# Second fp16 copies of attention probabilities on VectorE, and sample state products in 32-column groups, in a hybrid decoder layer

## The chip, the cores and the metric

The kernel runs on one core of one Trainium2 chip. The metric is the device time of one execution in microseconds (us). A core has five engines with an instruction stream each: TensorE (PE in the profile; its weight loads are PEld), VectorE (DVE), ScalarE (ACT), GpSimd (POOL) and SyncE (SP), which here issues the transfers. They meet only at semaphores.

## The reference

One inference step of a decoder layer for a prompt of 2048 tokens and for a sample batch of 8 sequences with 8 new tokens each.

```python
h = rmsnorm(x, norm_w)
z = h @ w_in
q, k, v, qb, kb, vb, g_lr, gate_a, gate_b = jnp.split(z, split_points(), axis=-1)
q = rope(rmsnorm(heads(q, H_A), q_norm_w), pos)
k = rope(rmsnorm(heads(k, H_A), k_norm_w), pos)
o_a = attend(q, k, v)             # 8 heads of 64, windows (128,1), (512,4), (2048,16), mixed by their denominators
log_a = jax.nn.log_sigmoid((g_lr @ w_gate_up + b_gate).astype(jnp.float32)) / GATE_TAU
o_b, s_fin = gla_chunked(...)     # 4 heads, keys of 64, values of 128
o_b = rmsnorm(o_b, gla_norm_w)
mixed = jnp.concatenate([o_a * silu(gate_a), o_b * silu(gate_b)], axis=-1)
y = x + mixed @ w_out
```

Two places in it matter for the change. In the attention of the prompt each query has a softmax, p = exp(s - m), and the product of p with the values. In the gated linear attention each head carries a state of 64 x 128, and one chunk does

```python
o = (jnp.einsum('bhts,bhsv->bhtv', scores, vc)
     + jnp.einsum('bhtk,bhkv->bhtv', qc * jnp.exp(b), state))
state = (jnp.exp(b_last)[..., None] * state
         + jnp.einsum('bhsk,bhsv->bhkv', kc * jnp.exp(b_last[:, :, None] - b), vc))
```

For the sample the chunk is the 8 new tokens, and each of the 8 sequences has states of its own, which come from and go back to device memory.

## The kernel before, in words

**Projections.** The input projection goes over 16 tiles of 128 prompt rows and a tile of 64 sample rows. Rows and weights are kept as two fp16 parts each, and a product is three matmuls for each 128 of the depth (lines L1628, L1316 and L1319). These matmuls are the bulk of TensorE's work, and they are also what stands between the steps of the attention.

**Attention of the prompt.** `attend` (L888) makes one unit of work: 128 queries of two heads (branches 1 and 2, window 128 by 1 and 512 by 4) or of four heads (branch 3). A unit has three steps. In `qk` TensorE makes scores (L901), VectorE masks them and takes the maximum (L909), and ScalarE takes the exponential (L912). In `tr` TensorE transposes the probabilities (L919) into PSUM, and `split` (L873) makes two fp16 parts of them, the rounded copy h and the remainder l. In `pv` TensorE multiplies both parts with the values (L934), and `added` (L945) joins the two halves of the result with ScalarE (L950) and VectorE (L951) and stores it.

**`split`** deals with its calls in turn. On an odd call ScalarE makes h (L878) and VectorE the remainder (L879), both from PSUM. On an even call ScalarE first copies the whole tile to SBUF as fp32 (L881), then h is made from that copy, and GpSimd makes the remainder (L886). That second h is made by ScalarE (L883), or by VectorE (L885) when the count of calls is a multiple of four. Since `added` raises the count by two, 72 of the 80 second copies go to ScalarE and 8, all of branch 3, to VectorE.

**The state of the sample.** `sample_gla` (L1816) works on two pairs of heads, p = 0 and 1. A pair's states of all 8 sequences lie in S0: 128 partitions (two heads of 64) by 8 sequences by 256 columns (the two heads' values, the blocks off the diagonal zero). The queries are spread into qxs, 72 columns for each sequence with 8 filled, so that any window of 64 columns holds one sequence's queries at its own place and zeros elsewhere. Eight matmuls (L1850) add up all sequences into O_s, 64 rows by 256; two small ones for each pair add the products within the chunk (L1856). For the new states GpSimd expands the values over the sequences (L1868, tile vx) and scales the old states (L1874); TensorE makes the updates U_s (L1878), two matmuls of 512 columns for each head, and VectorE adds them (L1882). The two heads of a pair use the two column halves of TensorE's array, since their results stand on partitions 0 to 63 and 64 to 127.

**The order.** No scheduler decides what stands where. `ORDER` (L52) lists for each engine the numbers of its instructions in the order in which they are to run, and `in_order` (L545) binds them in that order. So an engine that waits for one instruction holds up all that is listed behind it. The same TensorE stream holds attention, projections and gated linear attention, listed between each other. SyncE's list sets the order in which transfers are issued. The other work of the core that runs at the same time are the scores of the sample against its cache of keys: GpSimd multiplies (L1483) and VectorE reduces (L1484).

Of the kernel before, what the change touches and what calls it, by code (L numbers as in the profile page):

```python
# [7 lines left out]
F32 = mybir.dt.float32  # L8
# [4 lines left out]
AF = mybir.ActivationFunctionType  # L13
# [5 lines left out]
P = 128  # L19
# [6 lines left out]
NS = 64  # L26
# [534 lines left out]
def tile_hymba(ctx: ExitStack, tc: tile.TileContext, A: dict):  # L561
# [277 lines left out]
    with ExitStack() as c1:  # L839
# [33 lines left out]
        def split(out, in_, f):  # L873
# [6 lines left out]
            else:  # L880
                ACT.activation(f, in_, AF.Copy, scale=P_SCALE)  # L881
                if split_[0] % 4:
                    ACT.activation(h, f, AF.Copy)  # L883
                else:
                    DVE.tensor_copy(h, f)  # L885
# [1503 lines left out]
```

## Time and profile before

| | |
|---|---|
| time, median of 3 executions | 1237.86 us (1237.41 to 1240.5) |
| the profiled execution | 1238.56 us, of which the span of the trace is 1236.7 |
| mean granted clock of TensorE | 0.998 |
| TensorE busy | 1188.1 us (96%) |
| VectorE busy | 948.1 us (77%) |
| ScalarE busy | 817.6 us (66%) |
| GpSimd busy | 542.8 us (44%) |
| moved by DMA | 283.08 MB, 229 GB/s mean |
| second fp16 copies | 72 on ScalarE, from 149.6 to 712.4 us; 8 on VectorE, from 547.8 to 722.5 us |
| state products and updates of the sample | 762.5 to about 826 us |

Shares are of the whole span. The stages overlap, and each has its own limit, so a share of the span says little about a stage; the tables by stretch of time in the prediction do. Starts are given from the start of the span. A row of the trace names line, engine, operation, the tiles written and read, and shapes as partitions by elements. An fp32 matmul leaves two rows, so L1850's 16 matmuls are 32 rows and L1878's 8 are 16.

### The profile page before, as it was taken

Reading aid. Unit: us, or ns where it says so; the run is one execution under the profiler, and the core shown is the slowest. Engines: PE = TensorE matmul, PEld = TensorE weight load, DVE = VectorE, ACT = ScalarE, POOL = GpSimd, SP = SyncE. Lnnn points to the kernel's source line nnn. Section 1 sums busy time; section 2 is a strip of 40 time slices with the busy share of each in tenths; the row PEclk is TensorE's granted clock in tenths of the full one; section 3 lists DMA queues with packets and bytes.
Section 4 is the critical chain, followed back from the end, with each engine's and each line's share of the span. In section 5 each row is a group of like instructions: output and inputs, shape, how many; then the busy total and the mean of one; then the engine's idle time right before and its main releaser. Section 6 shows DMA issues by size and latency. Waiting matters only on the chain.

```text
span 1236.7 us, 26182 instructions
## 1 busy us (share of the span) xinstructions
PE 1188.1 (96%) x8942; PEld 717.8 (58%) x8942; DVE 948.1 (77%) x2458; ACT 817.6 (66%) x2183; POOL 542.8 (44%) x475
## 2 busy tenths in 40 slices
PE   5999999999999999999999999999999999999998
PEld 3444465566666656666777665645655665555543
DVE  7988788888988958668777675689999999833562
ACT  6555697889689968968866653568878865421220
POOL 0155443565647335552444466655535454401220
PEclk9999999999999999999999999999999999999999
DMA  8658946988856898789999876865773477899971
GB/s 292 231 171 240 232 144 163 239 214 207 199 175 165 208 248 283 229 234 267 269 247 260 252 232 209 233 196 177 233 250 95 155 245 237 284 348 370 401 275 49
DMA packets 235832, 283.08 MB, mean 229 GB/s; under 512 B 116193, under 2 KB 146866, under 8 KB 232626
## 3 DMA queue, kind: packets, MB, share of 16 engines
q1 hardware_dynamic: 235698, 281.40, 76.6%
q8 instruction: 71, 1.16, 0.4%
q14 instruction: 63, 0.52, 0.1%
HBM read 183.02 MB, written 75.24 MB: 209 GB/s over the span
## 4 chain that ended last, share of the span: by engine, by line
PE 57%; DVE 17%; ACT 11%; DMA 5%; issue 5%; POOL 2%; SPq 1%; POOLq 0%; DVEq 0%; ACTq 0%
PE Y L1974 10%; PE acc_v L1628 5%; PE acc_q L1628 4%; PE acc_k L1628 4%; PE acc_gb L1628 4%; PE t L919 3%; PE acc_qkb L1628 3%; PE O L934 3%; ACT p L912 3%; PE acc_vb L1628 3%; PE s L901 3%; PE acc_g L1628 3%; DVE p L909 2%; PE OS L2231 2%; PE sc_e L745 1%
## 5 line engine op out<-in xcount | busy, mean ns | idle before, releaser
L1483 POOL TENSOR_TENSOR pr<-k,qb 128x512 f32<-128x512 f32 x128 | 167.5, 1309 | 163.3 <-DVE sck L1484 73.0
L1628 PEld LDWEIGHTS <-hr 128*128 128x128 f16 x1824 | 172.6, 98 | 111.0 <-issue 10.8
L912 ACT ACTIVATE p<-p,o 128x256 f32<-128x256 f32 (+1 forms) x384 | 172.9, 455 | 24.3 <-DVE o L909 17.6
L1628 PEld LDWEIGHTS <-hl 128*128 128x128 f16 x1248 | 119.7, 98 | 119.1 <-issue 7.5
L1974 PE MATMUL Y<-w_o,mh 128*128 128x512 f16 x768 | 180.3, 379 | 0.1
L886 POOL TENSOR_TENSOR pt<-p,pt 128x512 f16<-128x512 f32 (+1 forms) x80 | 91.2, 1140 | 125.1 <-ACT pt L883 89.0
L934 PE MATMUL O<-v,pt 128*128 128x128 f16 x1200 | 134.7, 220 | 5.0 <-DVE o L951 1.6
L1484 DVE TENSOR_REDUCE sck<-pr 128x8 f32<-128x512 f32 x128 | 87.0, 680 | 49.8 <-POOL pr L1483 49.4
L919 PE MATMUL t<-ident,p 128*128 128x128 f32 x600 | 120.2, 279 | 4.9 <-ACT p L912 2.9
L1974 PEld LDWEIGHTS <-mh 128*128 128x128 f16 x768 | 72.3, 98 | 78.6 <-issue 4.9
L934 PEld LDWEIGHTS <-pt 128*128 128x128 f16 x1200 | 94.5, 99 | 36.7 <-POOL pt L886 3.8
L1628 PE MATMUL acc_q<-w_q,hl 128*128 128x512 f16 x384 | 109.5, 379 | 1.3 <-DVE vp L1283 1.2
L1628 PE MATMUL acc_g<-w_g,hr 128*128 128x272 f16 (+1 forms) x768 | 109.5, 277 | 0.9 <-DVE so_g L1170 0.6
L1628 PE MATMUL acc_v<-w_v,hl 128*128 128x512 f16 x384 | 109.6, 383 | 0.7 <-DVE vp L1283 0.7
L1628 PE MATMUL acc_k<-w_k,hl 128*128 128x512 f16 x384 | 108.6, 379 | 1.0 <-DVE vp L1283 0.7
L1628 PE MATMUL acc_vb<-w_vb,hr 128*128 128x512 f16 x384 | 95.1, 379 | 1.5 <-DVE so_g L1170 1.5
L909 DVE CUSTOM_DVE_ANT_0 p<-s,m3w,scl_s 128x128 f32<-128x128 f32 (+1 forms) x256 | 87.1, 395 | 11.3 <-DMA o_d<-o 5.0
L1628 PE MATMUL acc_gb<-w_gb,hr 128*128 128x512 f16 x384 | 93.8, 380 | 0.0
L919 PEld LDWEIGHTS t<-ident,p 128*128 128x128 f32 x600 | 75.3, 141 | 27.0 <-ACT p L912 12.8
L901 PE MATMUL s<-kk,qq 128*128 128x256 f16 (+1 forms) x512 | 84.8, 264 | 5.0 <-DVE o L909 2.0
L1628 PE MATMUL acc_qkb<-w_qkb,hr 128*128 128x512 f16 x288 | 81.5, 379 | 0.4 <-ACT zq L1248 0.4
L2016 POOL TENSOR_TENSOR oc<-oc 128x512 f32<-128x512 f32 x32 | 39.7, 1257 | 86.1 <-DVE oc L2009 68.2
(539 smaller groups left out, 2494.8 us busy)
## 6 DMA issues: line engine op xcount, KB each, us to landing
k<-in_cache_k_win SPq DMA_DIRECT2D x104, 256.0 KB
sv_b<-in_cache_v_win SPq DMA_DIRECT2D x24, 1024.0 KB
hr<-h_d SPq DMA_DIRECT2D x44, 512.0 KB
qb<-q_d SPq DMA_DIRECT2D x64, 256.0 KB
oc<-o_d SPq DMA_DIRECT2D x48, 264.0 KB
o_d<-o SPq DMA_DIRECT2D x64, 132.0 KB
x<-in_x_prompt SPq DMA_DIRECT2D x16, 512.0 KB
h_d<-hl SPq DMA_DIRECT2D x16, 512.0 KB
```

Source lines behind the costliest of these rows:

```text
L886: POOL.tensor_tensor(l, f, h, ALU.subtract)
L901: PE.matmul(s_ps[:, i * w : (i + 1) * w], q, k, start=(n == 0), stop=(n == len(prods) - 1),)
L909: DVE.tensor_tensor_reduce(s[:, sl], s_ps[:, sl], mask, neg, BIG, ALU.add, ALU.min, nmf(i))
L912: ACT.activation(s[:, sl], s[:, sl], AF.Exp, bias=nmf(i), scale=-1.0, accum_out=denf(i))
L919: PE.transpose(p_ps[:, i * P : (i + 1) * P], t["s"][:, i * P : (i + 1) * P], ident[:])
L934: PE.matmul(o_, t["pt"][:, c, (i * nb + b) * P : (i * nb + b + 1) * P], vf(i, b), start=(n == 0), stop=(n == 2 * nb - 1),)
L1483: POOL.tensor_tensor(pr[:], kt, qt, ALU.mult)
L1484: DVE.tensor_reduce(out, pr[:].rearrange("p (u k d) -> p u k d", u=2, k=4), AX.X, ALU.add)
L1628: PE.matmul(z, a_[:, k, :], w[:, p_, k, cols], start=(k == 0 and i == 0), stop=(k == KT - 1 and i == 2),)
L1974: PE.matmul(Y[:], a_[:, k, :], w_[:, part, k, :512], start=(i == 0), stop=(i == len(prods) - 1),)
L2016: eng.tensor_tensor(o_[g], o_[g], w[:, g].unsqueeze(2).to_broadcast([P, NH, HD]), ALU.mult)
L2231: PE.matmul(OS[32 * x : 32 * x + 32, 0:256], ps(x), vs_[bb][:, 256 * u : 256 * u + 256], start=(i == 0), stop=(i == 13),)
```

## The change

There are three parts. The number of matmuls stays as it is, and so does the set of transfers.

1. In `split` the second copy h is always made by VectorE. 72 copies (62 of 128x512, 10 of 128x256) go from ScalarE's list to VectorE's.
2. In `sample_gla` the state products write 32 rows in place of 64 (four sequences each), into column group 0 or 32 of the array, and neighbours alternate between the two. qxs is cut to 512 columns for each pair, which takes two small copies more. Both heads' expanded values are made first (two buffers for vx), and the updates U_s go over the column blocks outside and the heads inside, so that neighbours alternate between the array's halves; the additions follow them.
3. `ORDER` is replaced as a whole. On all five engines neighbours move past each other by a few places; which transfers there are and what they move is as before.

```diff
             else:
                 ACT.activation(f, in_, AF.Copy, scale=P_SCALE)
-                if split_[0] % 4:
-                    ACT.activation(h, f, AF.Copy)
-                else:
-                    DVE.tensor_copy(h, f)
+                DVE.tensor_copy(h, f)
                 POOL.tensor_tensor(l, f, h, ALU.subtract)
...
-            qxs = g1.tile([P, 2, 8, 72], F32, name="qxs")
+            qxs = g1.tile([P, 2, 512], F32, name="qxs")
             POOL.memset(qxs[:], 0.0)
             for p in range(2):
                 POOL.tensor_copy(
-                    qxs[:, p, :, 0:8], qe[:, p, :].rearrange("p (b t) -> p b t", t=8)
+                    qxs[:, p, :504].rearrange("p (b s) -> p b s", s=72)[:, :, 0:8],
+                    qe[:, p, :56].rearrange("p (b t) -> p b t", t=8),
                 )
+                POOL.tensor_copy(qxs[:, p, 504:512], qe[:, p, 56:64])
...
-                qxp = qxs[:, p].rearrange("p b s -> p (b s)")
-                for bt in range(8):
-                    PE.matmul(
-                        O[:NS, p * 256 : (p + 1) * 256], qxp[:, 64 * bt : 64 * bt + 64],
-                        S0[:, bt, :], start=(bt == 0), stop=False,
-                    )
+                for i in range(4):
+                    for g in range(2):
+                        bt, r0 = 4 * g + i, 32 * g
+                        PE.matmul(
+                            O[r0 : r0 + 32, p * 256 : (p + 1) * 256],
+                            qxs[:, p, 64 * bt + r0 : 64 * bt + r0 + 32],
+                            S0[:, bt, :], start=(i == 0), stop=False, tile_position=(0, r0),
+                        )
...
+                vxs = []
                 for j in range(2):
...
-                    vx = g1.tile([NS, 8, P], F32, name=f"vx_{h}", tag="vx", bufs=1)
+                    vx = g1.tile([NS, 8, P], F32, name=f"vx_{h}", tag="vx", bufs=2)
...
+                    vxs.append(vx)
...
+                for q in range(2):
+                    for j in range(2):
+                        h = 2 * p + j
+                        PE.matmul(
+                            Us[q][64 * j : 64 * j + 64], kdt[:NS, 0, 64 * h : 64 * h + 64],
+                            vxs[j][:, 4 * q : 4 * q + 4, :], start=True, stop=True,
+                        )
+                for j in range(2):
...
                     for q in range(2):
-                        PE.matmul(
-                            Us[q][js], kdt[:NS, 0, 64 * h : 64 * h + 64],
-                            vx[:, 4 * q : 4 * q + 4, :], start=True, stop=True,
-                        )
                         DVE.tensor_tensor(
```

Of `ORDER` these are two lines of TensorE's list; all others change in the same way.

```diff
-        "898-900 388-389 393-396 400-401 909-911 916-918 407-408 412 402 413 419 403 420 424 414 425 415 "
+        "898-900 388-389 393-396 400-401 909-911 916-917 407-408 412 402 413 419 403 918 420 424 414 425 "
```

What it moves is seen best in the engines' instruction lists. Lines shift a little: a row of L878, L881, L909, L912 or L951 before is L880, L883, L908, L911 or L950 after, and the cast on VectorE is L884. First ScalarE near 152 us, in the first units of branch 1. In a name like `pt_1_0_1_3_1` the first number is the branch, the last is the pair of heads in a group of four: a 0 is an odd call of `split`, a 1 an even one; p are probabilities, t their transpose in PSUM, o the result with maximum and denominator. Before:

```order
L878 ACTIVATE pt_1_0_0_1_0_1332<-t_1_0_0_1_0_1327 128x512
L912 ACTIVATE p_1_0_0_2_0_1339,o_1_0_0_2_1318<-p_1_0_0_2_0_1339,o_1_0_0_2_1318 128x256
L881 ACTIVATE p_1_0_0_1_1_1293<-t_1_0_0_1_1_1362 128x512
L912 ACTIVATE p_1_0_0_2_0_1339,o_1_0_0_2_1318<-p_1_0_0_2_0_1339,o_1_0_0_2_1318 128x256
L883 ACTIVATE pt_1_0_0_1_1_1367<-p_1_0_0_1_1_1293 128x512
L912 ACTIVATE p_1_0_0_2_1_1375,o_1_0_0_2_1318<-p_1_0_0_2_1_1375,o_1_0_0_2_1318 128x256 x2
L950 ACTIVATE ol_5_1358<-O_1_0_0_0_1319 128x256
```

And after, the same place:

```order
L880 ACTIVATE pt_1_0_0_1_0_1332<-t_1_0_0_1_0_1327 128x512
L911 ACTIVATE p_1_0_0_2_0_1339,o_1_0_0_2_1318<-p_1_0_0_2_0_1339,o_1_0_0_2_1318 128x256
L883 ACTIVATE p_1_0_0_1_1_1293<-t_1_0_0_1_1_1362 128x512
L911 ACTIVATE p_1_0_0_2_0_1339,o_1_0_0_2_1318<-p_1_0_0_2_0_1339,o_1_0_0_2_1318 128x256
L911 ACTIVATE p_1_0_0_2_1_1375,o_1_0_0_2_1318<-p_1_0_0_2_1_1375,o_1_0_0_2_1318 128x256 x2
L949 ACTIVATE ol_5_1358<-O_1_0_0_0_1319 128x256
```

The cast is gone from between the exponentials; all else stands as it did.

Then VectorE near 194 us. ra, rv and rs belong to the norm of a row tile, za to the projection of the sample rows. Before:

```order
L951 TENSOR_TENSOR o_1_0_1_2_2051<-O_1_0_1_2_2268,ol_45_2315 128x4x64
L631 TENSOR_TENSOR ra_x10_2234<-rr_x10_2233 128x1
L627 TENSOR_SCALAR rv_x11_2578<-ss_11_2574 128x1
L632 SCALAR_TENSOR_TENSOR ra_x10_2234<-ra_x10_2234,rv_x10_2232 128x1
L633 SCALAR_TENSOR_TENSOR rs_10_2231<-ra_x10_2234,rr_x10_2233 128x1
L1330 TENSOR_TENSOR za_0_2611<-za_0_2611,acc_q_s_2594 64x512
L879 SCALAR_TENSOR_TENSOR pt_2_0_1_0_0_2373<-t_2_0_1_0_0_2367,pt_2_0_1_0_0_2373 128x256
```

After:

```order
L884 CAST pt_1_0_1_3_1_2324<-p_1_0_1_3_1_2253 128x512
L633 TENSOR_TENSOR ra_x10_2234<-rr_x10_2233 128x1
L950 TENSOR_TENSOR o_1_0_1_2_2051<-O_1_0_1_2_2268,ol_45_2315 128x4x64
L629 TENSOR_SCALAR rv_x11_2578<-ss_11_2574 128x1
L634 SCALAR_TENSOR_TENSOR ra_x10_2234<-ra_x10_2234,rv_x10_2232 128x1
L1329 TENSOR_TENSOR za_0_2611<-za_0_2611,acc_q_s_2594 64x512
L635 SCALAR_TENSOR_TENSOR rs_10_2231<-ra_x10_2234,rr_x10_2233 128x1
L884 CAST pt_2_0_1_0_1_2410<-p_2_0_1_0_1_2332 128x256
L881 SCALAR_TENSOR_TENSOR pt_2_0_1_0_0_2373<-t_2_0_1_0_0_2367,pt_2_0_1_0_0_2373 128x256
```

Two casts came in, the combination of a unit's result moved behind a step of the norm, and the sum for the sample moved ahead of another.

Last TensorE at 762 to 776 us, the first pair of heads of the sample. S0 are the states, vx the expanded values, U_s00 and U_s01 the updates of sequences 0 to 3 and 4 to 7. Before, the products stand in two pieces, with the first head's updates between them:

```order
L1628 MATMUL acc_g1_13_12212<-w_g_6885,hr_13_11627 128x256
L1850 MATMUL O_s_9879<-S0_0_9880,qxs_9875 64x256 x2
L1878 MATMUL U_s00_9894<-vx_0_9896,kdt_smp_9871 64x512
L1878 MATMUL U_s01_9895<-vx_0_9896,kdt_smp_9871 64x512
L1850 MATMUL O_s_9879<-S0_0_9880,qxs_9875 64x256 x6
L1628 LDWEIGHTS hr_13_11627
```

After, the eight products stand together some 40 rows earlier (`O_s_9881<-S0_0_9882,qxs_9875 32x256 x8`), and the updates of both heads follow as below; before, the second head's updates stood some 60 rows behind the first's, each with an L1856 after it.

```order
L670 MATMUL ptg_e0_0_10026<-ident_79,zqk_e0_10013 128x128
L1885 MATMUL U_s00_9896<-vx_0_9898,kdt_smp_9871 64x512
L1885 MATMUL U_s00_9896<-vx_1_9901,kdt_smp_9871 64x512
L1859 MATMUL O_s_9881<-vb_s_9873,Ac_smp_9675 64x128
L1885 MATMUL U_s01_9897<-vx_0_9898,kdt_smp_9871 64x512
L1885 MATMUL U_s01_9897<-vx_1_9901,kdt_smp_9871 64x512
L1859 MATMUL O_s_9881<-vb_s_9873,Ac_smp_9675 64x128
```

The two heads' updates now stand next to each other. In the second pair of heads they don't: there the updates from vx_2 stand together, and those from vx_3 some 150 rows later, as before.

More of the change, by code (lines that the diff above doesn't have):

```diff
@@ L1876, in sample_gla @@
                     )
+                for q in range(2):
[6 more added lines that the diff above has]
+                for j in range(2):
+                    h = 2 * p + j
+                    js = slice(64 * j, 64 * j + 64)
+                    sd = S0[js, :, j * P : (j + 1) * P]
                     for q in range(2):
-                        PE.matmul(
-                            Us[q][js], kdt[:NS, 0, 64 * h : 64 * h + 64],
-                            vx[:, 4 * q : 4 * q + 4, :], start=True, stop=True,
-                        )
                         DVE.tensor_tensor(
```

886 rows, old and new, of the table ORDER are left out of this document.

## The prediction

> **What bounds the kernel now.** First the busy shares and the chain that ended last, from the page:
>
> ```profile
> PE 1188.1 (96%) x8942; PEld 717.8 (58%) x8942; DVE 948.1 (77%) x2458; ACT 817.6 (66%) x2183; POOL 542.8 (44%) x475
> PE 57%; DVE 17%; ACT 11%; DMA 5%; issue 5%; POOL 2%; SPq 1%; POOLq 0%; DVEq 0%; ACTq 0%
> ```
>
> TensorE carries most of the time, and ScalarE's and VectorE's shares of the chain (11% and 17%) say that in places they hold it up. Where, is seen in a table of busy time by stretch (start, end and length; busy time of PE, PEld, DVE, ACT and POOL with instructions; granted clock, DMA share, GB/s). The casts that the change moves run from 149.6 to 722.5 us, the sample's products in 760 to 830:
>
> ```profile
> 145.00:200.00 55.00, 50.91 (x442) 34.44 (x443) 46.08 (x165) 53.38 (x181) 21.88 (x20) 1.00 0.49 156
> 200.00:300.00 100.00, 99.79 (x704) 62.05 (x703) 85.24 (x220) 83.36 (x233) 57.08 (x44) 1.00 0.90 219
> 300.00:395.00 95.00, 95.00 (x726) 63.11 (x724) 82.69 (x202) 79.93 (x226) 56.23 (x43) 1.00 0.70 183
> 395.00:455.00 60.00, 53.53 (x404) 34.09 (x401) 44.38 (x127) 47.92 (x137) 22.13 (x17) 1.00 0.90 225
> 455.00:545.00 90.00, 89.49 (x731) 62.09 (x729) 66.08 (x215) 80.80 (x244) 49.10 (x41) 1.00 0.80 239
> 580.00:725.00 145.00, 142.63 (x1191) 102.89 (x1189) 104.79 (x357) 99.06 (x342) 67.07 (x53) 1.00 0.99 254
> 760.00:830.00 70.00, 68.00 (x392) 36.62 (x389) 48.54 (x82) 35.65 (x82) 41.30 (x32) 1.00 0.70 210
> ```
>
> So there are three kinds of stretch. In 145 to 200 ScalarE is full (53.38 of 55) and TensorE is not (50.91); in 395 to 455 TensorE misses 6.5 us. From 200 to 395 and from 455 to 545 TensorE has no gap worth naming (99.79 of 100, 95.00 of 95, 89.49 of 90): there nothing done for ScalarE can pay. In 760 to 830 TensorE is busy 68.0 of 70 and its own work is the time.
>
> All sums below stand against the profiled execution, 1238.56 us, which lies 0.70 above the median of 1237.86.
>
> **1. The casts leave ScalarE.** The rows of the two casts (duration as least/median/most), and ScalarE's cast by stretch:
>
> ```profile
> L883 ACT ACTIVATE pt<-p x72: 401/629/690, 149.6 to 712.4; 128x512 f16<-128x512 f32 x62, 128x256 f16<-128x256 f32 x10
> 145.00:200.00 55.00, 6.68 (x13) 1.00 0.49 156
> 200.00:300.00 100.00, 8.14 (x14) 1.00 0.90 219
> 300.00:395.00 95.00, 8.96 (x14) 1.00 0.70 183
> 395.00:455.00 60.00, 5.01 (x8) 1.00 0.90 225
> 455.00:545.00 90.00, 10.07 (x16) 1.00 0.80 239
> 580.00:725.00 145.00, 3.74 (x6) 1.00 0.99 254
> ```
>
> Together with one cast between 545 and 580 that is all 72. What ScalarE's lateness costs TensorE is in the waits of 145 to 200 (total, times, longest):
>
> ```profile
> PEld t L919 <- ACT p L912: 3.5, 10, 0.8
> PEld L934 <- POOL pt L886: 1.8, 6, 0.4
> PEld L934 <- ACT pt L878: 1.3, 4, 0.5
> PE t L919 <- ACT p L912: 1.1, 3, 0.6
> ```
>
> These are 7.7 us of waits on the weight load and the matmul, which partly lie over each other; TensorE's gap is 55.00 - 50.91 = 4.1. All stand behind ScalarE: the exponentials (L912) and first copies (L878) queue behind the casts, and POOL's subtraction (L886) waits for a cast. Taking 13 casts out frees 6.68 us of 53.38. The wait does not vanish, though. VectorE is busy 46.08 there and receives the 13: at the mean of its eight casts (0.60, below) for six pieces of 512 columns and some 0.35, an estimate from that, for seven of 256 (so many by the listed order), 6.0 us, so 52.1 of 55. The next bound is then VectorE at 52.1, 2.9 below the stretch. I take **-2.5**; the ends are -4.1 (the whole gap) and 0 (VectorE takes the wait over).
>
> In 395 to 455 eight casts (5.01) go, and TensorE's waits for ScalarE are:
>
> ```profile
> PEld t L919 <- ACT p L912: 2.2, 8, 0.4
> PEld L934 <- ACT pt L878: 1.5, 3, 0.9
> PEld t L919 <- ACT p L881: 1.3, 2, 0.8
> PE t L919 <- ACT p L881: 0.8, 2, 0.6
> PE O L934 <- ACT pt L878: 0.7, 1, 0.7
> ```
>
> That is 6.5 with overlaps, of which not all is the casts' doing: ScalarE is busy only 47.92 of 60 and also waits for others. 5.01 of 47.92 is a tenth of its work, so between 0.7 (a tenth of the waits) and 5.0 (every cast stood in front of a wait); I take **-1.7**, nearer to the tenth. In 580 to 725 only six casts are left: **-0.3**. Sum -4.5, between 0 and -9.
>
> **2. The casts land on VectorE.** The eight that it has already, then one of them beside what GpSimd did (start, duration):
>
> ```profile
> L885 DVE CAST pt<-p x8: 418/427/1000, 547.8 to 722.5; 128x512 f16<-128x512 f32 x8
> 597.13 1.00 DVE L885 CAST pt<-p 128x512 f16<-128x512 f32 x1
> 596.57 1.28 POOL L1483 TENSOR_TENSOR pr<-k,qb 128x512 f32<-128x512 f32 x1 [0.80 <-DVE sck L1484]
> ```
>
> Five took 418 to 427 ns; the three that began while GpSimd was in a product of L1483 took longer, the one quoted from 597.13 to 598.13, 0.28 after the product's end at 597.85. The eight sum to 4.8 us, 0.60 each. In 200 to 395 VectorE holds 85.24 + 82.69 = 167.9 of 195 and gets 28 casts: 28 x 0.60 = 16.8, so 184.7 or 95%. The ends are 28 x 0.42 = 11.8 and 28 x 1.00 = 28.0, and with the latter VectorE would be at 195.9 of 195. What covers the casts there is TensorE's projection matmuls, which the listed order puts between the attention steps. How loose that cover is, shows in TensorE's waits over 200 to 395, of which these are the largest two:
>
> ```profile
> PEld t L919 <- ACT p L912: 2.0, 7, 0.4
> PEld L934 <- DVE pt L879: 0.7, 2, 0.5
> ```
>
> VectorE was late twice, 0.7 us in all. What is queued behind a cast is the masks and maxima of the next scores (L909), then ScalarE's exponential, then the transposes, which are the first row. I take **+1.0**, about the size of what VectorE costs now; with the cover gone it is all of 16.8. In 455 to 545, 16 x 0.60 = 9.6 on top of 66.08 leaves VectorE at 84% and costs nothing.
>
> A rule of the Trainium skill speaks against this move: SBUF — State Buffer, section "SBUF: two separate sides", says that VectorE in a two-port mode and GpSimd share a pair of ports as an exclusive lock, which whoever starts first keeps for the whole instruction. The trace agrees (1.00 us against 0.42). By that rule a cast meets GpSimd with GpSimd's share of this stretch, (57.08 + 56.23) / 195 = 58%, and waits half a product, 0.64, so 0.42 + 0.37 = 0.79, and 28 of them 22 us in place of 16.8: still under the 27 that VectorE has free, so the sum stays and the first rival's chance rises.
>
> **3. The sample's state products in two column groups.** The rows of the two lines (least/median/most in ns) and the matmuls in time; then, from the sample attention later, the same shape in four column groups:
>
> ```profile
> L1850 PE MATMUL O_s<-S,qxs x32: 379/379/430, 762.5 to 811.5; 128*64 128x256 f32 x32
> L1878 PE MATMUL U_s<-vx,kdt_smp x16: 589/589/640, 763.5 to 825.3; 64*64 64x512 f32 x16
> 763.53 1.93 PE L1878 MATMUL U_s<-vx,kdt_smp 64*64 64x512 f32 x4
> 765.38 2.80 PE L1850 MATMUL O_s<-S,qxs 128*64 128x256 f32 x12
> 768.12 3.19 PE L1628 MATMUL acc_vb<-w_vb,hr 128*128 128x512 f16 x14
> 773.58 0.64 PE L1878 MATMUL U_s<-vx,kdt_smp 64*64 64x512 f32 x1
> 773.59 0.43 PE L1856 MATMUL O_s<-vb_s,Ac_smp 64*64 64x128 f32 x2
> 775.44 0.39 PE L1628 MATMUL acc_vb<-w_vb,hr 128*128 128x512 f16 x1
> 1094.66 1.91 PE L2231 MATMUL OS<-sv_b,P2x 128*32 128x256 f32 x32
> 1096.38 0.83 PE L2231 MATMUL OS<-sv_b,P3x 128*32 128x256 f32 x12
> ```
>
> Twelve rows of the state product take from 765.38 to 768.12, 0.23 each (each fp32 matmul leaves two rows). With neighbours in four column groups, 32 rows of the same 128x256 take from 1094.66 to 1096.38, 0.054 each. Two groups should be half as good as four, 0.108 (an estimate from that row). 32 x (0.23 - 0.108) = **-3.9**; the ends are 0 (no overlap) and 32 x (0.23 - 0.054) = -5.6.
>
> Updates: the first two matmuls (four rows) take 763.53 to 765.38, the other two 773.58 to 775.44, and the small products L1856 begin 0.01 after an update, in the other half: halves do run side by side here. Now all four of the first pair of heads stand together in alternating halves: 1.85 + 1.86 = 3.7 becomes some 1.86 plus what of L1856 sticks out (two pairs of rows of 0.43, half hidden), 2.3: **-1.4**, ends 0 and -1.9. In the second pair of heads the four updates stay apart by half, as the order rows show, and gain nothing. The zero fill is an eighth smaller and two copies of 8 columns come in on GpSimd, which no TensorE row waits for here: nothing. Together -5.3; TensorE being busy 68.0 of 70, most passes on, and I take **-4.8** for what later waits may keep.
>
> Against it stands the Trainium skill's TensorEngine Tiling (Array Packing), "Key Properties": a change of tiling mode drains TensorE. In the two lines' rows the longest is 0.05 above the usual (430 against 379, 640 against 589 ns), which I read as what a change of kind costs, and the visits stay about as many (fewer in the first pair of heads, more in the second), so by the rule too the sum moves by some 0.1.
>
> **4. The new orders.** They move neighbours past each other on all engines and add no work. Near 194 us, as the rows show, two casts stand in front of VectorE's next steps, and its combination L951 moves behind two short steps. Nothing in the trace prices this: nearest are the waits above, single ones of 0.4 to 0.9, so I take 0 with 2 us either way.
>
> **Sum:** -4.5 + 1.0 - 4.8 = -8.3, so 1238.56 - 8.3 = 1230.3, and 1229.6 beside the median; I say **1230**.
>
> **Rivals.**
> - *VectorE becomes the bound from 200 to 395.* Its 27.1 us without work are mostly waits for others' results, so new work does not simply fall into them. If they stay, the 16.8 appears in the time: 1238.56 - 9.3 + 16.8 = **1246**. For it: 95% busy and casts of up to 1.00. Against it: TensorE, full there, waits for VectorE 0.7 in 195, so the casts have a reserve. It decides when TensorE's waits on L879, L909 and the casts' subtraction grow by over 8 us there. Chance 0.13.
> - *ScalarE's wait only changes hands*, or what is won before 455 is lost from 580 on, where the DMA share is 0.99 and rows of the cache come no sooner: only the sample pays, 1238.56 - 4.8 = **1233.8**. For it: VectorE at 52.1 of 55. Against it: TensorE is busy 142.63 of 145 in that later stretch, so it and not the transfers fills the time. Chance 0.18.
> - *The sample's pairs do not overlap* or later waits eat them: -3.5 from the attention alone, **1235**. For it: two-group columns at full height appear in no row. Against it: the four-group rows. Chance 0.09.
>
> **How the numbers follow.** The forecast, with both halves paying, has 0.60 and spans 1222 to 1234. A measurement tells about 0.3% from no change, 3.7 us: faster is below 1234.1, slower above 1241.6. Faster is the 0.60 and half of the second rival, 0.69; slower the first rival less its mild cases, 0.12; the rest, 0.19, is the same. The range goes down to the forecast's own end with the larger bounds (-4.1, -3, -5.6, -1.9, and no price on VectorE: about -15, little of it likely in full) and up into the first rival: 1222 to 1243, which leaves out the upper part of that rival and a few hundredths below.
>
> **What would show it.** Right: L883 gone as a cast and 80 casts on VectorE at 0.5 to 0.8 mean; 145 to 200 shorter by 2 to 3 with ScalarE under 50; 200 to 395 unchanged with VectorE at 94 to 96%; the state products' rows starting in pairs within some 10 ns and taking 3.5 us in all. Wrong: rows in TensorE's waits from L879, L909 or L886 that were not there between 200 and 395; state products still 0.2 apart; or the gain before 455 present but gone again by 725.

## The result, and the profile after

The changed kernel takes 1245.59 us (median of 11 executions, 1242.89 to 1251.89) beside 1240.53 us for the kernel before in as many (1237.41 to 1243.57). The ratio is 1.0042, with a 95% interval of 1.0028 to 1.0056: **slower by some 5 us**, where 8 less were forecast. The profiled execution took 1242.89 us, of which the span is 1241.1.

The busy shares and the chain, as on the page of before:

```profile
PE 1185.8 (96%) x8942; PEld 715.4 (58%) x8942; DVE 972.6 (78%) x2530; ACT 786.0 (63%) x2111; POOL 542.0 (44%) x477
PE 27%; DVE 9%; ACT 4%; DMA 4%; issue 3%; POOL 3%; SPq 0%; POOLq 0%; DVEq 0%; ACTq 0%
```

The work moved as announced: ScalarE has 31.6 us less busy time, VectorE 24.5 more, TensorE 2.3 less; pairs of the sample's rows now lie over each other on TensorE. Where rows of one engine overlap, busy time counts the overlap once, so it changes by less than the casts' rows add up to (43.2 us on ScalarE before). The chain's shares add up to 50% of the span here and to 98% before, so they are not compared. The same stretches as before (start, end, length; PE, PEld, DVE, ACT, POOL busy; clock, DMA share, GB/s):

```profile
145.00:200.00 55.00, 51.28 (x452) 35.34 (x453) 48.97 (x183) 48.84 (x170) 21.39 (x20) 1.00 0.51 152
200.00:300.00 100.00, 98.64 (x690) 60.48 (x688) 90.40 (x218) 75.30 (x213) 57.09 (x43) 1.00 0.85 217
300.00:395.00 95.00, 94.73 (x708) 62.14 (x707) 86.22 (x223) 73.29 (x211) 55.72 (x43) 1.00 0.67 180
395.00:455.00 60.00, 52.72 (x396) 33.13 (x394) 48.36 (x133) 43.84 (x126) 19.17 (x15) 1.00 0.84 213
455.00:545.00 90.00, 86.22 (x681) 59.46 (x680) 67.38 (x206) 68.71 (x207) 48.39 (x39) 0.98 0.71 230
580.00:725.00 145.00, 140.22 (x1177) 100.41 (x1175) 108.35 (x354) 97.33 (x330) 63.79 (x51) 0.99 0.98 256
760.00:830.00 70.00, 69.19 (x433) 38.87 (x431) 48.63 (x87) 36.49 (x86) 45.67 (x41) 1.00 0.82 249
```

In 200 to 300 and in 455 to 545, where TensorE had no gap (99.79 and 89.49), it now has 1.4 and 3.8 us of them. ScalarE is down in every stretch that has casts, from 53.38 to 48.84 in the one where it had been full. TensorE shows 0.4 us more there, but not from the casts: before, a wait of 1.9 us that ended at 145.98 reached into the stretch, and from 149.6 us, where the casts begin, to 200 TensorE has 46.80 busy, 47.29 before. VectorE is at 91% from 200 to 395 (90.40 + 86.22 of 195), not at the 95% of the forecast. The casts themselves cost about what was expected of them. This is their line (least/median/most in ns), and then VectorE's time in it from 200 to 395:

```profile
L884 DVE CAST pt<-p x80: 277/421/1595, 149.2 to 733.0; 128x512 f16<-128x512 f32 x70, 128x256 f16<-128x256 f32 x10
```

```profile
200.00:300.00 100.00, 9.00 (x14) 1.00 0.85 217
300.00:395.00 95.00, 7.80 (x15) 1.00 0.67 180
```

9.00 + 7.80 = 16.8, the very figure of the forecast (28 casts at 0.60; e1 below has 17.1). What was wrong is what that does to TensorE.

**Where the time went** is best seen by setting each TensorE instruction's start in one trace against that of the same instruction in the trace of before (they can be paired, since the instructions are the same and only their places differ). The median of these differences around some points of before's time, in us (a positive number is late), for the change and for the experiments below:

| kernel | 145 | 200 | 300 | 395 | 470 | 545 | 600 | 740 | 790 | 850 | 1200 |
|---|---|---|---|---|---|---|---|---|---|---|---|
| the change | -0.9 | -0.9 | 1.3 | 1.7 | 6.9 | 8.7 | 9.1 | 10.5 | 6.1 | 4.6 | 4.4 |
| e1 casts alone | -1.1 | 0.4 | 3.4 | 4.9 | 8.6 | 12.1 | 12.9 | 16.8 | 17.3 | 17.3 | 17.4 |
| e5 idle reductions | 0.3 | 6.3 | 9.2 | 11.0 | 14.5 | 17.8 | 20.3 | 21.5 | 21.4 | 21.4 | 22.1 |
| e9 casts to 200 | -0.4 | 0.2 | 0.0 | 0.0 | -0.2 | -0.2 | 0.0 | 6.6 | 5.9 | 5.9 | 6.0 |
| e2 sample alone | -1.2 | -0.9 | -0.9 | -0.9 | -0.7 | 0.0 | 0.0 | 2.8 | 2.2 | 4.9 | 5.3 |
| e3 casts back | 1.3 | 2.5 | 3.0 | 3.5 | 5.3 | 6.5 | 6.5 | 8.1 | 4.4 | 2.9 | 2.3 |
| e4 one cast ahead | 0.6 | 2.3 | 4.6 | 5.8 | 11.1 | 13.2 | 13.5 | 13.8 | 10.2 | 8.7 | 8.1 |
| e7 old, then new | -0.9 | -0.6 | -0.6 | -0.6 | 0.1 | 1.1 | 0.7 | 3.3 | -0.5 | -2.0 | -2.0 |
| e10 new, then old | 1.4 | 1.6 | 4.2 | 5.2 | 9.6 | 10.5 | 11.7 | 14.6 | 15.3 | 15.3 | 16.0 |
| e17 casts, old, then new | -1.0 | 0.2 | 3.2 | 4.8 | 9.7 | 13.2 | 14.1 | 16.0 | 12.2 | 10.7 | 10.5 |
| e13 fp32 copy left out | -0.4 | 0.1 | -0.3 | -1.1 | -1.5 | 1.6 | 3.3 | 5.1 | 5.5 | 5.6 | 9.5 |
| e15 remainders left out | -2.1 | -1.9 | -2.4 | -2.4 | -2.6 | -3.1 | -2.8 | -1.4 | -0.4 | -0.4 | 0.2 |

Each row is one trace, and traces of one program differ: e9 runs the very instructions of before in the same order from 200 us on, keeps level to 600, and then loses 6 us up to 740 (the DMA share is 0.99 from 580 to 725). So this table tells where, and the medians of many executions tell how much. In the changed kernel's row the loss of 11 us lies between 200 and 740 us, in many small steps and one large one near 459 us, and the sample (760 to 830) gives 6 back.

The large step, in the changed kernel's trace: TensorE, then VectorE, GpSimd and ScalarE in the same few microseconds (start, duration, in brackets the idle time before and what ended it).

```profile
456.36 0.38 PE L1627 MATMUL acc_qkb<-w_qkb,hr 128*128 128x512 f16 x1
459.00 0.29 PE L933 MATMUL O<-v,pt 128*128 128x128 f16 x1 [2.25 <-DVE pt L884]
459.07 0.63 PE L1627 MATMUL acc_qkb<-w_qkb,hr 128*128 128x512 f16 x1
```

```profile
457.92 0.69 DVE L1483 TENSOR_REDUCE sck<-pr 128x8 f32<-128x512 f32 x1 [2.99 <-POOL pr L1482]
458.52 0.42 DVE L884 CAST pt<-p 128x512 f16<-128x512 f32 x1
```

```profile
456.62 1.26 POOL L1482 TENSOR_TENSOR pr<-k,qb 128x512 f32<-128x512 f32 x1 [16.73 <-DMA k<-in_cache_k_win]
```

```profile
454.46 0.60 ACT L883 ACTIVATE p<-t 128x512 f32<-128x512 f32 x1
```

The cast's input, ScalarE's fp32 copy, was ready at 455.06. VectorE could not begin it, since a reduction of the sample's scores stands ahead of it in the list; that waits for GpSimd's product, and this for keys of the cache, which had only just landed. Before, the same reduction waited too, but the cast was on ScalarE:

```profile
453.20 0.69 DVE L1484 TENSOR_REDUCE sck<-pr 128x8 f32<-128x512 f32 x1 [1.49 <-POOL pr L1483]
```

The sample, in the changed kernel's trace:

```profile
771.38 1.92 PE L1852 MATMUL O_s<-S,qxs 128*32 128x256 f32 x16
773.23 1.70 PE L1627 MATMUL acc_g<-w_g,hr 128*128 128x256 f16 x14
776.49 1.08 PE L1885 MATMUL U_s<-vx,kdt_smp 64*64 64x512 f32 x4
778.47 0.38 PE L1859 MATMUL O_s<-vb_s,Ac_smp 64*64 64x128 f32 x2
778.78 1.69 PE L1627 MATMUL acc_vb<-w_vb,hr 128*128 128x512 f16 x7
```

Sixteen rows of the state product run from 771.38 to 773.23, 0.116 each (0.23 before), and the first pair's updates with their L1859 from 776.49 to 778.78, 2.29 us (3.7 before, for the updates alone).

### The profile page after: what moved, and what is told of

It is laid out like the page before. It is cut to its first block, busy times and chain, and to the rows that moved or that the text cites. A ratio compares the mean times of both kernels' runs of the same rounds, so it can differ in the third digit from the quotient of the medians.

```text
span 1241.1 us, 26131 instructions
## 1 busy us (share of the span) xinstructions
PE 1185.8 (96%) x8942; PEld 715.4 (58%) x8942; DVE 972.6 (78%) x2530; ACT 786.0 (63%) x2111; POOL 542.0 (44%) x477
## 4 chain that ended last, share of the span: by engine, by line
PE 27%; DVE 9%; ACT 4%; DMA 4%; issue 3%; POOL 3%; SPq 0%; POOLq 0%; DVEq 0%; ACTq 0%
PE Y L1986 9%; PE acc_gb L1627 4%; PE acc_vb L1627 3%; PE OS L2243 2%; PE acc_g L1627 2%; PE sc_e L747 1%; POOL pr L1482 1%; DMA k<-in_cache_k_win 1%; DMA qb<-q_d 1%; DMA vb_d<-vbs 1%; ACT qbd L706 1%; PE tm L1951 1%; DVE so_g L1177 1%; PE O L1799 1%; PE O L1793 1%
## 5 line engine op out<-in xcount | busy, mean ns | idle before, releaser
L911 ACT ACTIVATE p<-p,o 128x256 f32<-128x256 f32 (+1 forms) x384 | 172.8, 452 | 47.3 <-DVE o L908 35.9
L885 POOL TENSOR_TENSOR pt<-p,pt 128x512 f16<-128x512 f32 (+1 forms) x80 | 93.9, 1173 | 126.8 <-DVE pt L884 107.0
L908 DVE CUSTOM_DVE_ANT_0 p<-s,m3w,scl_s 128x128 f32<-128x128 f32 (+1 forms) x256 | 87.7, 393 | 7.0 <-DMA o_d<-o 2.7
```

The costliest lines, as they stand in the source:

```text
L885: POOL.tensor_tensor(l, f, h, ALU.subtract)
L908: DVE.tensor_tensor_reduce(s[:, sl], s_ps[:, sl], mask, neg, BIG, ALU.add, ALU.min, nmf(i))
L911: ACT.activation(s[:, sl], s[:, sl], AF.Exp, bias=nmf(i), scale=-1.0, accum_out=denf(i))
```

## The experiments

The theory after the result: the casts themselves cost (A), as a load on VectorE that makes everything behind them late. Its rivals: the new orders cost and the casts are covered (B); or the casts cost by their own lateness or by the lock with GpSimd, not by load. Where a kernel takes "the orders of before up to 742 us", each engine's list is cut at a place up to which both lists hold the same instructions, so that the two parts fit. Each ratio is to the kernel before on the same chip. A gain or loss in us is the ratio's.

### e1: the casts alone

```diff
-                if split_[0] % 4:
-                    ACT.activation(h, f, AF.Copy)
-                else:
-                    DVE.tensor_copy(h, f)
+                DVE.tensor_copy(h, f)
```

> The kernel before with part 1 alone: the 72 casts go to VectorE, each behind the same neighbour as in the changed kernel; all other orders and the sample as before. Theory A (the casts on VectorE are what costs: they fill it or stand behind its waits): the loss of 10 us that TensorE's stream shows between 145 and 760 us comes back nearly whole, 1.006 to 1.009 of before. Theory B (the new orders cost, the casts themselves are covered or pay): 0.997 to 1.002.

Measured: 1255.65 us, 1.011 (1.009 to 1.0131), 11 to 16 us lost. That is theory A, and more than it said. Its stretches:

```profile
145.00:200.00 55.00, 49.91 (x440) 34.39 (x439) 49.70 (x175) 48.03 (x166) 21.33 (x20) 1.00 0.49 148
200.00:300.00 100.00, 97.86 (x686) 60.16 (x685) 91.26 (x224) 74.62 (x212) 56.50 (x42) 1.00 0.83 212
455.00:545.00 90.00, 86.57 (x684) 59.07 (x683) 70.53 (x205) 70.35 (x210) 46.90 (x38) 1.00 0.76 236
```

TensorE lost time in all of them, also in 145 to 200, where ScalarE was relieved, and in 455 to 545, where VectorE has only 78% of the time. What grew are TensorE's waits for VectorE. Two of them from 200 to 560 us in the kernel before (the third and fourth row below have no more than 0.2 there), and then four in e1 (L879 before and L880 in e1 are the odd calls' remainder, L909 and L907 the masks and maxima):

```profile
PE s L901 <- DVE o L909: 1.7, 3, 1.1
PEld L934 <- DVE pt L879: 0.7, 2, 0.5
```

```profile
PE s L899 <- DVE o L907: 3.4, 8, 0.6
PEld L932 <- DVE pt L880: 3.3, 5, 1.4
PE O L932 <- DVE pt L880: 2.1, 3, 1.2
PE acc_k L1626 <- DVE vp L1281: 1.4, 2, 0.7
```

None of the four is a cast: it is VectorE's other work that comes late. The waits for the casts themselves are 0.6 us there, and 2.3 with overlaps in 145 to 200. The longest row, the transposes' wait for the exponentials, went from 5.4 to 7.3.

Half clock behind a gap (see the end) is in some of the traces, but it is not what the time went to: the one execution of e1 with a granted clock of 1.0 all through took 1255.39 us, and the four of before with 1.0, on other chips, 1239.79 to 1242.76.

### e5: the load without the casts

```diff
                 if split_[0] % 4:
                     ACT.activation(h, f, AF.Copy)
+                    dm = sm.tile([P, 8], F32, name=f"dm_{split_[0]}", tag="dm", bufs=1)
+                    DVE.tensor_reduce(dm[:], f.rearrange("p (a b) -> p a b", a=8), AX.X, ALU.add)
```

> The kernel before with 72 reductions of the fp32 copy (128x512 or 128x256 into 8 numbers that nobody reads) on VectorE, at the very places where the casts alone stood; the casts stay on ScalarE. They load VectorE with some 0.68 us each (the rows of L1484 have that shape and take 0.68) and nothing waits for them. Load (what stands behind on VectorE comes late): the loss of the casts alone comes back, 1.008 to 1.015. Dependency (the cast's own result is late, or the lock with GpSimd costs): 0.999 to 1.003.

Measured: 1257.85 us, 1.0117 (1.0092 to 1.0142), as much as the casts. The line of the reductions, and TensorE's waits from 200 to 560 us (L883 is here the odd calls' remainder, L915 the masks and maxima):

```profile
L889 DVE TENSOR_REDUCE dm<-p x72: 405/676/687, 151.7 to 734.7; 128x8 f32<-128x512 f32 x62, 128x8 f32<-128x256 f32 x10
```

```profile
PE s L907 <- DVE o L915: 4.5, 9, 1.4
PEld L940 <- DVE pt L883: 4.0, 5, 1.3
PE O L940 <- DVE pt L883: 2.6, 3, 1.2
```

Nobody reads these results, ScalarE keeps its casts, and no reduction lasts longer than 687 ns, so neither a late copy nor a wait for GpSimd's ports is needed. 46 us of rows on VectorE (38.8 more busy time) cost 14.5 us of the kernel's time, and the same waits came up as in e1. **So load alone can cost this much.** Load takes in the place in the list: like the casts, the reductions hold up what is behind them while they wait for ScalarE's copy (ten times, 4.6 us in all; the casts of e1 12 times, 5.4). The trace also puts three waits of GpSimd, 5.8 us in all, down to a reduction. The 6 us that the row of e5 loses between 145 and 200 are in part the clock's, 0.94 in that stretch of this trace, the slowest of the six executions.

### e9: only the stretch where ScalarE was full

```diff
-                if split_[0] % 4:
+                if split_[0] % 4 and tag not in EARLY:
```

`EARLY` names the 13 units up to 199 us; up to there the orders are the changed kernel's.

> The kernel before with the changed kernel's orders up to about 199 us and the 13 casts of that stretch on VectorE; all the rest, the other 59 casts and the sample included, as before. The forecast's first step (ScalarE is the bound there): 2.5 us gained, 0.997 to 0.999. Rival (the wait only changes hands): 0.9995 to 1.002.

Measured: 1242.96 us, 1.0001 (0.9984 to 1.0018). The stream is level with before at 200 us (0.2, then 0.0 to 395). With the casts on VectorE in their place, the relief of ScalarE bought nothing even there.

### e13, e16 and e15: relief of one engine without load on another

e13 leaves out the fp32 copy, and with it the remainder (GpSimd subtracts the rounded copy from itself):

```diff
+                if split_[0] % 4:
+                    ACT.activation(h, in_, AF.Copy, scale=P_SCALE)
+                    POOL.tensor_tensor(l, h, h, ALU.subtract)
+                    return
                 ACT.activation(f, in_, AF.Copy, scale=P_SCALE)
...
```

> The kernel before, with the fp32 copy L881 left out in the 72 calls: ScalarE writes the fp16 copy straight from PSUM in the place of L883, and GpSimd subtracts it from itself, so that the remainder is left out of the result. ScalarE loses 72 x 0.59 = 42 us, VectorE and all orders stay. If ScalarE is what holds TensorE in 145 to 200 and 395 to 455, as the forecast had it: 0.994 to 0.998. If the next engine takes the wait over: 0.999 to 1.001.

Measured: 1245.47 us, 1.0035 (1.0021 to 1.0048), slower, and outside of both expectations. The stream is 1.5 us ahead at 470 and loses from there. Between 395 and 560 us the transposes (L917) wait for the copy (L879), which now is what frees their PSUM, and only at its place in the list:

```profile
PEld t L917 <- ACT pt L879: 6.5, 7, 1.5
PE t L917 <- ACT pt L879: 4.5, 7, 1.3
```

So the kernel as a whole says little. In one trace, up to 470 us, some 23 us less busy time on ScalarE (278.17 to 254.99 from 145 to 470) gain 1.5, with copies that come later than before.

e16 leaves out the second fp16 copy in place of the fp32 copy; both products read the rounded copy, so that the remainder is left out and the rounded copy counts twice:

```diff
-                ACT.activation(f, in_, AF.Copy, scale=P_SCALE)
+                ACT.activation(f, in_, AF.Copy, scale=P_SCALE / 2 if split_[0] % 4 else P_SCALE)
                 if split_[0] % 4:
-                    ACT.activation(h, f, AF.Copy)
+                    POOL.tensor_tensor(l, f, f, ALU.add)
...
-                            o_, t["pt"][:, c, (i * nb + b) * P : (i * nb + b + 1) * P], vf(i, b),
+                            o_, t["pt"][:, 1 if t["one"] else c, (i * nb + b) * P : (i * nb + b + 1) * P], vf(i, b),
```

> The kernel before with the second fp16 copy on ScalarE (L883) left out in the 72 calls: GpSimd writes the rounded copy in place of the remainder, with the same instruction on other operands, and both products read it, so that the remainder is left out of the result. PSUM is released as before, ScalarE loses 72 x 0.60 = 43 us, and VectorE gets nothing. If ScalarE is what holds TensorE in 145 to 200 and 395 to 455: 0.994 to 0.998. If relief of ScalarE is worth nothing because VectorE and GpSimd end at the same time: 0.999 to 1.001.

Measured: 1249.51 us, 1.0075 (1.0049 to 1.01), outside of both. From 145 to 395 us the products (L932) wait for GpSimd (L880), on the weight load 6.6 us where before has 1.8:

```profile
PEld L932 <- POOL pt L880: 6.6, 7, 2.9
PE O L932 <- POOL pt L880: 4.7, 5, 2.4
```

The first of the two products now needs GpSimd, which the copy had spared it. It is not a clean relief, and nothing is concluded from it.

e15 takes work from VectorE: the odd calls' remainders are left out, and their products read the rounded copy twice:

```diff
             if split_[0] % 2:
                 ACT.activation(h, in_, AF.Copy, scale=P_SCALE)
-                DVE.scalar_tensor_tensor(l, in_, P_SCALE, h, ALU.mult, ALU.subtract)
...
-                            o_, t["pt"][:, c, (i * nb + b) * P : (i * nb + b + 1) * P], vf(i, b),
+                            o_, t["pt"][:, 0 if t["one"] else c, (i * nb + b) * P : (i * nb + b + 1) * P], vf(i, b),
```

> The kernel before, with the 80 remainders L879 on VectorE left out (the odd calls' products read the rounded copy twice, so the remainder is left out of the result). VectorE loses some 80 x 0.65 = 52 us, ScalarE and all orders stay. If VectorE's load is what holds TensorE, as the idle reductions say: 0.990 to 0.997, more than the relief of ScalarE gives. If VectorE has room before and only more load hurts: 0.998 to 1.001.

Measured: 1239.66 us, 0.9978 (0.9963 to 0.9992), between the two expectations: 40.5 us less busy time on VectorE gain 2.7 (1.0 to 4.6), and 38.8 more cost 14.5 in e5. So the kernel before had little to win from VectorE and much to lose from it; for ScalarE, e9 and the first part of e13 say that there was little to win.

### e4: one cast ahead of one reduction

```diff
+L884 CAST pt_1_3_0_0_1<-p_1_3_0_0_1 128x512
 L1483 TENSOR_REDUCE sck_1<-pr_2_1_3 128x2x4
-L884 CAST pt_1_3_0_0_1<-p_1_3_0_0_1 128x512
```

> The changed kernel with one single cast (of pt_1_3_0_0_1) moved ahead of the reduction L1483 that stands before it in VectorE's list and waits for keys of the cache. Waiting in line: TensorE's gap of 2.25 us before 459 us and the half clock behind it (some 1.5 us) go, and the time falls by 3 to 4 us against the changed kernel, to 1.001 to 1.002 of before. Load (VectorE is simply too full): one place makes no difference, 1.004.

Measured: 1244.91 us, 1.0028 (1.0009 to 1.0047), where the changed kernel has 1.0042: the intervals overlap, so the total does not tell it. The trace does at that place:

```profile
461.91 0.43 DVE L884 CAST pt<-p 128x512 f16<-128x512 f32 x1 [0.16 <-ACT p L883]
```

The cast begins 0.16 us after its input, the gap of 2.25 and the half clock behind it are gone, and between 450 and 470 us the stream loses 0.7 (10.4 to 11.1) in place of 3.3 (3.6 to 6.9). In what is left stands a wait of 1.04 for GpSimd's subtraction. So one place in the list was worth some 2.6 us in its stretch. From 395 to 470 together, though, the two traces lose as much (5.3 and 5.2): ahead of the place, where the orders are the same, e4's loses 2.7 more. Whether the 2.6 reach the end is not shown.

### e2 and e7: the sample alone, in old and in new orders

e2 is the kernel before with the new `sample_gla`, its own instructions placed as in the change:

```diff
+sample_gla: part 2 of the change
 ORDER: as before, but for the sample's own rows
```

> The kernel before with part 2 alone: the sample's products and updates with their own instructions placed as in the changed kernel, everything else in the order of before. Both theories: the stream of TensorE gained 6.0 us over the sample in the changed kernel, so 0.9945 to 0.997. If the gain were taken back by waits behind it, 0.998 to 1.001.

Measured: 1243.32 us, 1.0008 (0.9994 to 1.0022): nothing gained. TensorE's rows were as short as in the change, but from 780 to 840 us it then stood still for others; three of its rows in e2 with the wait in brackets (in the trace of before the first waits 0.46, the second not at all and the third 1.04):

```profile
787.77 0.44 PE L668 MATMUL ptg_e<-ident,zqk_e 128*128 128x128 f32 x2 [1.92 <-DVE la_e L689]
828.47 1.67 PE L1628 MATMUL acc_gb<-w_gb,hr 128*128 128x512 f16 x7 [1.65 <-DVE so_gb L1170]
835.12 0.69 PE L745 MATMUL sc_e<-qbd,kq_e 128*64 128x64 f32 x16 [2.32 <-POOL kq_e L712]
```

e7 takes the new orders too, from 742 us on:

```diff
+sample_gla: part 2 of the change
 ORDER to 742 us: as before
+ORDER from 742 us: as in the change
```

> The kernel before with the new sample, in the orders of before up to about 742 us and in the changed kernel's orders from there on; all casts as before. If the sample's gain of 5.7 to 6.0 us, which the streams of the changed kernel and of the one with the casts given back both show from 740 us on, belongs to the new sample in its new surroundings: 0.994 to 0.997. If it was only time lost before and caught up there: 0.998 to 1.001.

Measured: 1234.32 us, 0.9939 (0.9918 to 0.996). **This beats both kernels**, by 7.6 us the one before. In its trace two of the three waits are there, shorter in sum:

```profile
786.80 0.44 PE L668 MATMUL ptg_e<-ident,zqk_e 128*128 128x128 f32 x2 [1.88 <-DVE la_e L689]
830.36 0.69 PE L745 MATMUL sc_e<-qbd,kq_e 128*64 128x64 f32 x16 [1.37 <-POOL kq_e L712]
```

In e2's trace the granted clock fell behind the first and the third wait (0.58 from 788 to 792 and 0.57 from 836 to 840), which added to its loss; but an execution of e2 with a clock of 1.0 all through took 1244.7 us, and one of e7 1232.34.

### e3, e10 and e17: the other combinations

e3 is the change with the 72 casts on ScalarE; e10 has the casts and the new orders up to 742 us and then the kernel before; e17 has the casts in the old orders up to 742 us and then the changed kernel.

```diff
 e3:  casts as before   ORDER to 742 us: new      sample and ORDER behind: new
 e10: casts on VectorE  ORDER to 742 us: new      sample and ORDER behind: as before
 e17: casts on VectorE  ORDER to 742 us: as before  sample and ORDER behind: new
```

> The changed kernel with the 72 casts given back to ScalarE, each behind the neighbour that it had before; new orders and the new sample stay. Theory A: the loss goes, the sample's gain stays, 0.994 to 0.998 of before. Theory B: the loss stays, 1.003 to 1.006.

> The changed kernel's orders and casts up to about 742 us, and from there the old sample in the orders of before: the mirror of the kernel that took the old orders first. If the parts add up (some 10 us lost before 742, 6 gained behind): 1.007 to 1.010. If the sample's gain needs no other attention and the loss was less than one trace shows: 1.003 to 1.006.

> The casts on VectorE in the orders of before up to about 742 us (as in the kernel with the casts alone), then the new sample in the changed kernel's orders: the changed kernel without its new orders ahead of 742 us. If the parts add up, the casts' 13 to 14 us and the sample's 7 to 8: 1.004 to 1.006, as the changed kernel, and the new orders ahead of 742 are worth nothing. If they win back a part of what the casts cost: 1.008 or more.

Measured: e3 1241.75 us, 1.0007 (0.999 to 1.0023), between the two expectations; e10 1255.75 us, 1.0114 (1.0097 to 1.013), above the expectation; e17 1249.24 us, 1.0077 (1.0055 to 1.0098), between the two. As a table of ratios:

| up to 742 us | kernel before behind | new sample and orders behind |
|---|---|---|
| casts on ScalarE, old orders | 1 | 0.9939 (e7) |
| casts on ScalarE, new orders | | 1.0007 (e3) |
| casts on VectorE, old orders | 1.011 (e1) | 1.0077 (e17) |
| casts on VectorE, new orders | 1.0114 (e10) | 1.0042 (the change) |

In each row with both entries the new sample with its orders gains: 0.6%, 0.3% and 0.7%. With the casts on ScalarE the new orders of the attention cost 0.7% (e3 against e7); that they were made for the casts' other place may be why, which is not shown. With the casts on VectorE they change nothing in the left column and gain 0.35% in the right one. The parts do not add up to better than 0.3%, and which of the two holds is left open.

## Why the prediction was wrong, step by step

**The sum.** It started from an execution of 1238.56; the median of the kernel before is 1240.53, and 2 us of the miss are that. Beyond it, -8.3 was forecast and +5.1 measured, 13.4 apart. Steps 1 and 2 came out 17.2 worse (-3.5 forecast, +13.7 in e1). Steps 3 and 4 came out some 3.6 better with the casts on VectorE (-4.8 forecast, -8.4 from e1 to the change), and hid a part of it.

**Step 1, ScalarE's relief, forecast -4.5: failed.** It read a full engine (53.38 of 55) as the one that holds TensorE, and TensorE's whole gap of 4.1 as that engine's doing; 1.0 of it was the end of the wait up to 145.98, ahead of the first cast. e9 gave ScalarE just that relief and gained 0 (at most 2 by its interval); e13, up to 470 us, 1.5. The text had the reason itself, "the next bound is then VectorE at 52.1", and then still took most of the room between them. In e1 VectorE's busy time in that stretch was 49.70, not 52.1, and TensorE's 49.91: no engine was full any more, and the stretch was no shorter. Work that passes through two or three engines in turn did not run here up to 100% of the next.

**Step 2, the casts on VectorE, forecast +1.0: this is the step that failed most.** Steps 1 and 2 together were -3.5; e1 measured +13.7 for them (1.011 of 1241.26). The prices of the casts were right (6.0 us forecast for the 13 up to 200, 5.82 in the change and 6.00 in e1; 16.8 from 200 to 395). For the 13 that is partly luck: six wide casts took 0.42 where 0.60 was reckoned, and seven narrow ones 0.47 where 0.35 was. The sentence that failed is "VectorE was late twice, 0.7 us in all", taken as the measure of the reserve. Waits tell how late an engine was, not how much later it may be. And "leaves VectorE at 84% and costs nothing" failed too: VectorE was at 78% from 455 to 545 in e1, whose stream lost 3.5 us from 470 to 545 alone. e5 shows that load alone is enough: 0.3 us of the kernel for each us of rows on VectorE.

The rule of the Trainium skill that was weighed (SBUF — State Buffer, "SBUF: two separate sides") agrees with single casts, the longest of which took 1595 ns, ending 0.15 us after a GpSimd product, beside a median of 421. The mean of 0.79 that was reckoned by the rule for 200 to 395 was too high: it was 0.60 there (16.8 for 28), and 20 of all 80 casts took over 500 ns. The lengthening is a part of the casts' load, in e1 some 14 of their 46.4 us (an estimate, with 0.42 and 0.28 us for the two widths alone); but the reductions of e5 lasted 405 to 687 ns and cost as much, so the lock is not needed for such a loss.

**Step 3, the sample, forecast -4.8: right in its price, right in its sum only with new orders.** Forecast were 0.108 per row and 2.3 us for the first pair's updates; measured 0.116 and 2.29. Of "most passes on" the orders decide: nothing of it in e2, 7.6 us in e7 (5.0 to 10.2 by its interval), where these rows save 5.0. Whether the new orders gain more than let that pass is not shown; e7's trace gains 5.3 from 740 to 850.

**Step 4, the new orders, forecast 0 with 2 either way: too narrow.** By e3 against e7 they cost 0.7% up to 742 us while the casts are on ScalarE, and by e2 against e7 they gain 0.7% behind it. They were read for what stands where, and not for what they wait for.

**The rivals.** The first came close in its time (1246 against 1245.6), with chance 0.13, and that is mostly luck: VectorE did cost some 14 us, but not by being full from 200 to 395, where TensorE's stream in e1 lost 4.5. By its own sign, over 8 us more of TensorE's waits on L879, L909 and the subtraction there, it failed: these are 0.9 us before, 1.5 in the change and 2.9 in e1. The loss lies in all of 145 to 740, and the new sample took a third to two thirds of it back (4 to 9 us, by the rows of the table). That the wait changes hands (the second rival) is true of step 1. The range, 1222 to 1243, ended below the measured median.

## What to carry to other kernels

Busy shares under 100% and short waits do not show room on an engine: a kernel with idle work of the planned size in the planned places, and one with that much work left out, tell what a move is worth, and here, on VectorE, the first cost 14.5 us and the second gained 2.7. A move to a busy engine puts the work behind all that stands in that engine's list, and behind what that waits for; look at the instruction just ahead of the new place. And the parts of a change with orders of its own should be timed apart: the sample with the orders behind it is worth 0.6% here, and the whole was slower. The Trainium skill says of ScalarE and VectorE (Perfetto Trace Analysis, "Optimizing Scalar/DVE Operations") that work which either can do may go from a saturated VectorE to ScalarE; the runs agree with it read backwards, for work moved to VectorE, and already where VectorE then was busy 78 to 91% of a stretch (e1).

## What the runs showed of the hardware

- Half the clock after a gap. The row at 459.07 takes 0.63 for 512 columns, where 0.38 is usual; the granted clock is 0.50 from 459 to 461 and 0.70 from 461 to 463. That cost at most 1.6 us on top of the gap of 2.25 (an estimate: half of 2 us and 0.3 of 2 us). A gap of 1.86 before 448.18 in the same trace and one of 2.29 before 455.00 in e4's had no such effect, while in e2 waits of 1.92 and 2.32 had. So the length of the gap alone does not decide it here, and what does was not tested.
- Column groups. fp32 rows of 256 columns come every 0.23 us one after the other, every 0.116 in two column groups of 32 (this change) and every 0.054 in four (the sample attention of before).
- From 600 to 740 us, with a DMA share of 0.99 in most of it, two executions of the same instructions in the same order (e9 and before) differ by 6 us. It is one pair of traces; the executions of before lie within 6.2 us.
